# A two-block denoiser layer on one core: S5 kernel matrices turned where they are read, table copies moved to ScalarE, the last states copied by VectorE alone

## The chip, the core and the metric

The kernel runs on one core of a Trainium2 chip: TensorE (PE, matrix products), VectorE (DVE), ScalarE (ACT), GpSimd (POOL) and SyncE (SP), each with an instruction queue of its own that is worked off in order. SP does no arithmetic and only issues DMA transfers; ACT and POOL issue some too, and such an issue stands in their queue like any other instruction. The metric is the time of one execution on the device in microseconds (us).

## The reference, cut to what matters

Two blocks on 256 tokens of width 1024, float32 throughout. The first has two layers, latent attention (MLA) and an S5 state-space layer on 256 context and 256 latent tokens; the second block (attention and a gated convolution) follows and is left out here, since the change does not touch it.

```python
def _mla_mixer(h_lat, h_ctx, ...):          # layer 0: h = x * (1 + sc) + sh, then h @ w_in
    q_dn, kv_dn, k_rope, gate = split(h @ w_in)
    ...

def _s5_direction(u_ctx, u_lat, lam, dt, bmat, cmat):
    lam_bar = jnp.exp(lam * dt[:, None])
    b_bar = ((lam_bar - 1.0) / lam)[..., None] * bmat
    powers = jnp.exp(lam_dt[None] * jnp.arange(1, S5_CHUNK + 1))
    def step(h, u_chunk):
        bu = jnp.einsum('btgs,gps->btgp', u_chunk, b_bar)
        _, xs = lax.associative_scan(_ssm_combine, (a, bu), axis=1)   # x_t = lam_bar x_{t-1} + bu_t
        xs = xs + powers[None] * h[:, None]
        y = jnp.einsum('btgp,gsp->btgs', xs, cmat).real
        return xs[:, -1], y
    ...                                     # context first, its last state starts the latent tokens

def _s5_mixer(...):                         # layer 1, u, g = split(h @ w_in); 128 groups of 16 channels
    y = d_skip * u + forward direction + backward direction
    y = jax.nn.gelu(y)
    ya, yb = split(y @ w_glu + b_glu)
    return ((ya * sigmoid(yb)) * silu(g)) @ w_out
```

## The kernel before, in words

Large products are made either plainly in float32 (PE reads `raw`, the loaded weight) or as three products of split operands: ACT casts the weight to `whi` (L240), DVE subtracts to get `wlo` (L284), and PE takes hi*hi, hi*lo and lo*hi. Weights come from HBM in pieces of 512 KB into three rotating buffers each (`raw`, `whi`, `wlo`).

**Start (0 to 60 us).** The modulation vectors come from `in_wmod` (PE rows `b<-s,x`); DVE scales the tokens with them (`ready`, L483, eight instructions per half of the width); PE then makes the first columns of `h @ w_in` (`half`, rows `a<-s,raw` for the plain one and `a<-s,whi`, `a<-s,wlo` for the split ones). Beside that the tables of S5 are made: `tables()` reorders powers of `lam_bar` into `Em` (L988/L989, four copies on ACT) and `Fm` (L991/L992, four copies of 64x512 on POOL), and L993 copies `L4`. The list `HALVES` is the hand-written order of PE, SP and ACT in this stretch: "T0" calls `tables()` and then `ready(0)`, a number is a quarter of the products, "B" a part of the second half's modulation, "X" loads the second half of the tokens and "T1" makes it ready.

**S5 (about 530 to 789 us).** Time is cut into blocks of 4 tokens, so that the scan has 64 steps; within and between blocks the work is made of matrix products. Per m (0 to 15, eight groups each):

- *sums*: `inputs` makes u (PE `a<-s,raw`), ACT copies it to `Ub` (L1173) and writes it to HBM (`ud`), POOL reads it back as `U`; PE multiplies it with `BT` (`a<-U,whi`) and ACT copies the result to `Sc` (L1209, context) and to the `s` tiles (L1213, latent). DVE runs a tree over `Sc` (rows `sc<-LA,Sc` and `Sc<-Sc,sc`).
- *scan*: for each of four units, 63 steps on DVE (`ss<-x,s`, then twice `s<-s,ss`).
- *direct*: the part of y within a block. `s5_toeplitz` writes eight pieces of kernel matrices to HBM (`Td<-Kd`, issued by POOL). `kernel(m)` then loads 128x256 of it (`Ul<-Td`, POOL), ACT turns its two inner axes (`Ysb<-Ul`, L1339) and writes it back (`To<-Ysb`, issued by ACT). `direct(m)` loads u (`Ul<-ud`, SP) and two 64x4x64 blocks of `To` (SP) into one of two block-diagonal tiles `Tz` (named `x` in the profile) and PE multiplies (`c<-Ul,x`).
- *outputs*: two edge columns (L1256/L1257) and two copies of 64x16x63 states (L1262 forward, L1263 backward) into `H`, which is a `whi` buffer, three in all; PE multiplies with `CC` (`c<-whi,wlo`); for each pair of m ACT copies `Yb` (L1273) and writes it to HBM. `S5_DVE` says for which m the L1263 copy is made by DVE.
- *gates*: PE `b<-s,raw`, ACT `sg` (SiLU), written to HBM. *y(b)*: POOL loads `hl<-yd` once four m are done, ACT applies GELU and casts (`s<-hl`), DVE subtracts. *glu*: PE `a<-hl,raw` for the first three plainly, then split products (`a<-s,whi`), which fill the time from 789 us on.

`S5_PLAN` is the order in which these are written down; in S5 a scheduler at build time places each instruction in its engine's queue from that, by what is free when, so a change in one place moves others.

Of the kernel before, what the change touches and what calls it, by code (L numbers as in the profile page):

```python
# [19 lines left out]
P = 128  # L20
D = 1024
# [44 lines left out]
ORD = ("p", "d", "s")  # L66
KS = (0, 0)
KVP = True
HALVES = ("T0", "K4", 0, "B", 1, "B", 2, "B", 3, "X", "B", "T1")
S5_LATE = 16  # L70
LATE_AT = ()
SL1 = 1
# [10 lines left out]
S5_SPLIT = range(2, 8)  # L83
GLU_PLAIN = 3
GLU_EARLY = 6
S5_DVE = range(14, 16)
S5_UNITS = ((0,), (1,), (2,), (3,))

S5_PLAN = [("sums",0),("sums",1,(0,38)),("sums",2,(0,25),(1,25)),("sums",3,(1,25),(2,25)),("direct",0,4),("gates",0,5),("outputs",0,4),("scan",(1,13),(3,13)),("direct",4,8),("gates",5,13),("outputs",4,8),("direct",8,12),("scan",(2,38),(3,38)),("y",0,2),("gates",13,16),("outputs",8,12),("direct",12,16),("scan",(3,12)),("y",2,3),("glu",0,2),("outputs",12,16),("y",3,4),("glu",2,6)]
# [118 lines left out]
class Builder:  # L208
# [147 lines left out]
    def scratch(self):  # L356
        d = lambda shape, n: self.t(self.dp, shape, F32, n)
        self.BTd = d([16, P, 1024], "BTd")
        self.CCd = d([16, P, 1024], "CCd")
        self.Kd = d([P, 16, 112], "Kd")  # L360
        self.Td = d([P, 64, 64], "Td")
        self.To = d([P, 64, 64], "To")
        self.FEd = d([P, 2304], "FEd")
        self.LAd = d([P, 24, P], "LAd")
        self.sgd = d([16, P, NL], "sgd")
        self.ud = d([P, 16, 4, P], "ud")
        self.yd = d([P, 16, 4, 64], "yd")
# [101 lines left out]
    def mla_in(self):  # L469
# [7 lines left out]
        def ready(hf):  # L477

            kts = range(4 * hf, 4 * hf + 4)
            for kt in kts:  # L480
                for r in range(2):
                    sl = slice(r * NL, (r + 1) * NL)
                    nc.vector.tensor_scalar(xT[:, kt, sl], xT[:, kt, sl], self.sc(self.mod0, kt, r), self.sh(self.mod0, kt, r),  # L483
                                            op0=ALU.mult, op1=ALU.add)
            for kt in kts:
                self.h_last = self.split(hh[:, kt], hl[:, kt], xT[:, kt])
# [22 lines left out]
        with self.in_order(*ORD):  # L509
            fm = [self.mod_first(hf) for hf in range(2)]  # L510
            self.keep_busy(self.ones[256], KS[0])
            for _ in range(4):
                next(fm[0])
                self.keep_busy(self.ones[256], KS[1])
            load(0)
            for op in HALVES:
                if op == "T0":
                    next(fm[0])
                    self.tables()
                    ready(0)  # L520
                elif op == "B":
                    next(fm[1])
                elif op[:1] == "K" if isinstance(op, str) else False:
                    self.keep_busy(self.ones[256], int(op[1:]))
                elif op == "X":
                    load(1)
                elif op == "T1":
                    next(fm[1])
                    ready(1)
                else:  # L530
                    half(first[op], op, 0, KVP and op == 0)
# [386 lines left out]
    def s5_factors(self, keep, pre):  # L918
# [64 lines left out]

        f, b = slice(0, 64), slice(64, 128)
        gs = lambda x: x.rearrange("p s g -> p g s")
        def tables():
            for ri in range(2):
                nc.scalar.copy(Em[f, ri], gs(Lp[f, ri]))  # L988
                nc.scalar.copy(Em[b, ri], gs(Lp[b, ri, ::-1]))  # L989
            for ri in range(2):  # L990
                nc.gpsimd.tensor_copy(Fm[f, ri], gs(Q[f, ri, ::-1]))  # L991
                nc.gpsimd.tensor_copy(Fm[b, ri], gs(Q[b, ri]))  # L992
            nc.scalar.copy(L4, Lp[:, :, 3])  # L993
        L4 = self.t(keep, [P, 2, P])
        self.tables = tables
        return FE, L4
# [137 lines left out]
    def s5(self):  # L1134
# [98 lines left out]
        def direct(m):  # L1233

            if m % 2 == 0:
                pys["x"] = self.ps("c", (P, 2, 4, 64))
            py = pys["x"][:, m % 2]
            Ul = self.t(l1, [P, 4, 64], F32, "Ul", 3)
            nc.sync.dma_start(out=Ul, in_=udr[:, 4 * m:4 * m + 4, 0:64])
            T = Tz[m % TZ]  # L1240
            for j in range(2):
                rw = slice(64 * j, 64 * j + 64)
                nc.sync.dma_start(out=T[rw, :, rw], in_=self.To[rw, 4 * m:4 * m + 4])
            for q in range(4):
                self.mm(py[:, q], T[:, q], Ul[:, q], m % 2 == 0 and q == 0, False)
            pys[m] = pys["x"]

        def outputs(m):
# [10 lines left out]
            for x, D in enumerate(S):  # L1259
                n = D.shape[1]  # L1260
                k = min(n, 63 - n * x)
                nc.scalar.copy(H[f, :, :, 1 + n * x:1 + n * x + k], hv(D[f, :k, :, g]))  # L1262
                copy(H[b, :, :, 63 - n * x - k:63 - n * x], hv(D[b, k - 1::-1, :, g]))  # L1263
            py = pys.pop(m)
            for q in range(4):
# [46 lines left out]
        def sums(m0, m1):  # L1312
            for m in range(m0, m1):
# [11 lines left out]
                        n = 8 // len(TPM)  # L1325
                        self.s5_toeplitz(0, 16, range(n * i, n * i + n))
                yield from chunk_sums(m)
                for k in range(2 * m - 8, 2 * m - 6):
                    if 0 <= k < 16:
                        kernel(k)  # L1330

        def kernel(m):

            q = slice(4 * m, 4 * m + 4)
            a = self.t(l1, [P, 4, 64], F32, "Ul", 3)
            o = self.t(l1, [P, 4, 64], F32, "Ysb", 2)
            with self.tc.issue_after(self.u_read):
                nc.gpsimd.dma_start(out=a, in_=self.Td[:, q])
            nc.scalar.copy(o.rearrange("p q (o t) -> p q t o", t=4), a.rearrange("p q (t o) -> p q t o", t=4))  # L1339
            nc.scalar.dma_start(out=self.To[:, q], in_=o)  # L1340

        def take(it, n=1):
            for _ in range(n):
# [519 lines left out]
```

## Time and profile before

| | |
|---|---|
| time, median of 3 (lowest to highest) | 1420.02 us (1419.73 to 1423.65) |
| profiled execution: time, span in the trace | 1422.31 us, 1420.5 us |
| mean granted TensorE clock | 0.978 of 2.4 GHz |
| busy: PE, PEld | 1352.2 us (95%), 1151.5 us (81%) |
| busy: DVE, ACT, POOL | 1055.3 us (74%), 825.5 us (58%), 104.2 us (7%) |
| chain that ended last | PE 75%, ACT 8%, DMA 7%, DVE 6% |
| ... of it by line | DMA Ul<-Td 1%, ACT whi L1262 1%, ACT whi L1263 1% |

The span is the time from the first to the last recorded instruction; 1.8 us of the profiled execution lie outside it. PEld is TensorE's loading of weights, which overlaps its products. The chain is the work that ended last, followed back from the end: shares say on what the time hung, not how busy an engine was.

### The profile page before, as it was taken

The numbers are of one execution on the slowest core, as the hardware profiler recorded it, in microseconds if no ns is written. First come the engines' busy times: TensorE is split into PE (matmuls) and PEld (weight loads), VectorE is DVE, ScalarE is ACT, GpSimd is POOL, SyncE is SP. The second block draws the span as 40 slices with busy tenths as digits, with TensorE's granted clock in tenths as the row PEclk, the third lists the DMA queues.
The fourth block names the chain that finished last, engine by engine and source line by source line (L and its number), as shares of the span: only waits on it lengthen the run. The fifth ranks groups of instructions, "written<-read, shape, count | busy, mean of one in ns | idle before, by whom it ended". The sixth has DMA issues, their size and how long they took to land.

```text
span 1420.5 us, 26374 instructions
## 1 busy us (share of the span) xinstructions
PE 1352.2 (95%) x10042; PEld 1151.5 (81%) x10042; DVE 1055.3 (74%) x2546; ACT 825.5 (58%) x1429; POOL 104.2 (7%) x154
## 2 busy tenths in 40 slices
PE   5899999999999999888988999999999999999999
PEld 1577777877787666446877899999879999899999
DVE  7879768988689949899993465556667777688853
ACT  4598756665556943436368644445568664566642
POOL 3012100000011223210000000000100000000000
PEclk9999999999999989998999999999999999999999
DMA  8646533144275459764866766665433435565564
GB/s 310 223 164 223 186 126 117 56 130 145 82 263 184 151 159 313 212 190 139 245 207 203 251 206 191 198 187 180 158 116 122 146 126 163 171 185 180 184 186 135
DMA packets 105487, 252.60 MB, mean 178 GB/s; under 512 B 37168, under 2 KB 45744, under 8 KB 104976
## 3 DMA queue, kind: packets, MB, share of 16 engines
q1 hardware_dynamic: 77056, 204.50, 45.0%
q0 software_dynamic: 7344, 25.04, 5.7%
q10 hardware_dynamic: 20960, 21.37, 4.6%
q8 instruction: 79, 1.29, 0.4%
q14 instruction: 48, 0.39, 0.1%
HBM read 218.88 MB, written 34.08 MB: 178 GB/s over the span
## 4 chain that ended last, share of the span: by engine, by line
PE 75%; ACT 8%; DMA 7%; DVE 6%; issue 2%; ACTq 0%; SPq 0%; POOL 0%; POOLq 0%; DVEq 0%
PE a L228 59%; PE b L228 11%; PE c L228 2%; DMA ud<-Ub 1%; DMA s<-in_wmod 1%; ACT whi L240 1%; DMA Ul<-Td 1%; DVE wlo L284 1%; ACT whi L1262 1%; DVE bt L284 1%; PE c L669 1%; DMA raw<-in_w_glu 1%; ACT whi L1263 1%; ACT zc L1097 1%; DMA U<-ud 1%
## 5 line engine op out<-in xcount | busy, mean ns | idle before, releaser
L228 PE MATMUL a<-s,whi 128*128 128x256 f32 (+2 forms) x3024 | 645.1, 310 | 2.7 <-ACT whi L240 2.7
L228 PEld LDWEIGHTS a<-s,whi 128*128 128x128 f32 x3024 | 493.8, 191 | 34.3 <-issue 4.3
L228 PE MATMUL a<-s,wlo 128*128 128x256 f32 (+1 forms) x1512 | 464.1, 309 | 0.1
L284 DVE TENSOR_TENSOR wlo<-raw,whi 128x1024 fp32r<-128x1024 f32 (+2 forms) x234 | 280.8, 1201 | 195.3 <-ACT whi L240 192.7
L240 ACT CAST whi<-raw 128x1024 fp32r<-128x1024 f32 (+2 forms) x234 | 240.8, 1031 | 249.3 <-PE a L228 178.4
L228 PEld LDWEIGHTS a<-s,wlo 128*128 128x128 f32 x1512 | 289.0, 191 | 14.7 <-issue 0.9
L228 PE MATMUL a<-s,raw 128*128 128x512 f32 (+2 forms) x272 | 110.9, 559 | 17.6 <-ACT s L1213 6.5
L228 PEld LDWEIGHTS a<-s,raw 128*128 128x128 f32 x272 | 53.7, 203 | 64.3 <-issue 37.7
L284 DVE TENSOR_TENSOR s<-s,ss 128x64 f32<-128x64 f32 x504 | 88.8, 225 | 2.8 <-DVE s L284 0.2
L284 DVE TENSOR_TENSOR bt<-x,bc 128x512 f32<-128x512 f32 x128 | 83.5, 692 | 1.2
L228 PE MATMUL a<-x,whi 128*128 128x256 f32 (+1 forms) x384 | 74.2, 294 | 0.0
L284 DVE TENSOR_TENSOR ss<-x,s 128x128 f32<-128x128 f32 x248 | 63.1, 288 | 1.2
L228 PE MATMUL b<-s,raw 128*128 128x256 f32 x256 | 62.4, 404 | 1.3 <-ACT sg L1280 1.3
L228 PEld LDWEIGHTS a<-x,whi 128*128 128x128 f32 x384 | 60.4, 192 | 0.6
L228 PEld LDWEIGHTS b<-s,raw 128*128 128x128 f32 x256 | 51.0, 203 | 9.4 <-ACT sg L1280 1.7
L228 PE MATMUL a<-x,wlo 128*128 128x256 f32 (+1 forms) x192 | 56.1, 292 | 0.0
L284 DVE TENSOR_TENSOR sc<-LA,Sc 128x1024 f32<-128x1024 f32 (+5 forms) x96 | 44.3, 503 | 12.0 <-ACT Sc L1209 11.6
L284 DVE TENSOR_TENSOR Sc<-Sc,sc 128x1024 f32<-128x1024 f32 (+5 forms) x96 | 48.3, 503 | 0.4
L228 PEld LDWEIGHTS a<-U,whi 64*64 64x64 f32 x1024 | 32.3, 140 | 19.2 <-ACT Ub L1173 8.5
L731 DVE TENSOR_REDUCE st<-b 128x1 f32<-128x512 f32 (+1 forms) x64 | 34.8, 550 | 16.8 <-PE b L228 16.5
L228 PE MATMUL a<-U,whi 64*64 64x128 f32 x1024 | 37.5, 287 | 9.6 <-ACT Ub L1173 6.2
L240 ACT CAST s<-s 128x512 fp32r<-128x512 f32 (+1 forms) x48 | 25.9, 546 | 21.5 <-DVE s L284 15.0
(384 smaller groups left out, 2265.7 us busy)
## 6 DMA issues: line engine op xcount, KB each, us to landing
raw<-in_w_glu SPq DMA_DIRECT2D x64, 512.0 KB, 3.5
raw<-in_w_up SPq DMA_DIRECT2D x42, 512.0 KB, 3.5
raw<-in_w_out SPq DMA_DIRECT2D x40, 512.0 KB, 3.6
raw<-in_wmod SPq DMA_DIRECT2D x32, 512.0 KB, 3.6
raw<-in_w_u SPq DMA_DIRECT2D x32, 512.0 KB, 4.0
s<-in_wmod SPq DMA_DIRECT2D x16, 512.0 KB, 7.7
raw<-in_w_in SPq DMA_DIRECT2D x16, 512.0 KB, 4.2
BTd<-BT ACTq DMA_DIRECT2D x16, 512.0 KB, 3.4
```

Source lines behind the costliest of these rows:

```text
L228: self.last = self.ins(self.nc.tensor.matmul(out, l, r, start=start, stop=stop))
L240: self.nc.scalar.copy(hi, src)
L284: return self.ins(self.nc.vector.tensor_tensor(out, a, b, op=op))
L669: nc.tensor.transpose(pt[:, k, tt], pl[tt][:, (2 * b + k) * P:(2 * b + k + 1) * P], self.ident)
L731: nc.vector.tensor_reduce(st[:, 0:1], ps, axis=AX.X, op=ALU.max)
L1097: nc.scalar.copy(zt[f, :, 4:7], ct[f, :, 0:3])
L1262: nc.scalar.copy(H[f, :, :, 1 + n * x:1 + n * x + k], hv(D[f, :k, :, g]))
L1263: copy(H[b, :, :, 63 - n * x - k:63 - n * x], hv(D[b, k - 1::-1, :, g]))
```

## The change

Three edits. (1) `tables` takes a half: the `Em` copies stay at "T0"; the four `Fm` copies go from POOL to ACT and, with `L4`, to a new entry "F" of `HALVES` after the second quarter. (2) `kernel(m)` and the HBM tensor `To` go; `direct(m)` loads 128x256 of `Td` into `Ysb` (SP, two buffers), and two ACT copies of 64x4x4x16 turn it straight into the two diagonal blocks of `Tz`. (3) `S5_DVE` grows from m = 14, 15 to 12 to 15, and the forward copy obeys it as well, so all eight state copies of the last unit are on DVE.

```diff
-HALVES = ("T0", "K4", 0, "B", 1, "B", 2, "B", 3, "X", "B", "T1")
+HALVES = ("T0", "K4", 0, "B", 1, "F", "B", 2, "B", 3, "X", "B", "T1")
-S5_DVE = range(14, 16)
+S5_DVE = range(12, 16)
-        self.To = d([P, 64, 64], "To")
@@ mla_in
-                    self.tables()
+                    self.tables(0)
                     ready(0)
+                elif op == "F":
+                    self.tables(1)
@@ s5_factors
-        def tables():
+        def tables(hf):
             for ri in range(2):
-                nc.scalar.copy(Em[f, ri], gs(Lp[f, ri]))
-                nc.scalar.copy(Em[b, ri], gs(Lp[b, ri, ::-1]))
-            for ri in range(2):
-                nc.gpsimd.tensor_copy(Fm[f, ri], gs(Q[f, ri, ::-1]))
-                nc.gpsimd.tensor_copy(Fm[b, ri], gs(Q[b, ri]))
-            nc.scalar.copy(L4, Lp[:, :, 3])
+                if hf:
+                    nc.scalar.copy(Fm[f, ri], gs(Q[f, ri, ::-1]))
+                    nc.scalar.copy(Fm[b, ri], gs(Q[b, ri]))
+                else:
+                    nc.scalar.copy(Em[f, ri], gs(Lp[f, ri]))
+                    nc.scalar.copy(Em[b, ri], gs(Lp[b, ri, ::-1]))
+            if hf:
+                nc.scalar.copy(L4, Lp[:, :, 3])
@@ direct(m)
             T = Tz[m % TZ]
+            k = self.t(l1, [P, 4, 64], F32, "Ysb", 2)
+            nc.sync.dma_start(out=k, in_=self.Td[:, 4 * m:4 * m + 4])
             for j in range(2):
                 rw = slice(64 * j, 64 * j + 64)
-                nc.sync.dma_start(out=T[rw, :, rw], in_=self.To[rw, 4 * m:4 * m + 4])
+                nc.scalar.copy(T[rw, :, rw].rearrange("p q (o t) -> p q t o", t=4), k[rw].rearrange("p q (t o) -> p q t o", t=4))
@@ outputs(m)
-                nc.scalar.copy(H[f, :, :, 1 + n * x:1 + n * x + k], hv(D[f, :k, :, g]))
+                copy(H[f, :, :, 1 + n * x:1 + n * x + k], hv(D[f, :k, :, g]))
                 copy(H[b, :, :, 63 - n * x - k:63 - n * x], hv(D[b, k - 1::-1, :, g]))
@@ sums
-                for k in range(2 * m - 8, 2 * m - 6):
-                    if 0 <= k < 16:
-                        kernel(k)
-        def kernel(m):
-            q = slice(4 * m, 4 * m + 4)
-            a = self.t(l1, [P, 4, 64], F32, "Ul", 3)
-            o = self.t(l1, [P, 4, 64], F32, "Ysb", 2)
-            with self.tc.issue_after(self.u_read):
-                nc.gpsimd.dma_start(out=a, in_=self.Td[:, q])
-            nc.scalar.copy(o.rearrange("p q (o t) -> p q t o", t=4), a.rearrange("p q (t o) -> p q t o", t=4))
-            nc.scalar.dma_start(out=self.To[:, q], in_=o)
```

How the queues change at three places, word for word (line, operation, output<-input with buffer numbers, shape, count).

**Start, ACT.** Before, from the last `Em` copy to the second weight cast (`s_48` are the scaled tokens, `whi` the first quarters' weights):

```order
L989 COPY x_110<-x_148 64x512
L993 COPY x_188<-x_148 128x256
L240 CAST s_49_190<-s_48_189 128x512 x4
L240 CAST whi_284<-raw_282 128x512
L240 CAST whi_308<-raw_306 128x512
```

In the changed kernel, the same stretch:

```order
L995 COPY x_109<-x_147 64x512
L240 CAST s_48_189<-s_47_188 128x512 x4
L240 CAST whi_278<-raw_276 128x512
L991 COPY x_109<-x_168 64x512
L992 COPY x_109<-x_168 64x512
L991 COPY x_109<-x_168 64x512
L992 COPY x_109<-x_168 64x512
L997 COPY x_187<-x_147 128x256
L240 CAST whi_307<-raw_305 128x512
```

The four `Fm` copies now stand on ACT between the first and the second weight cast, behind the casts of the tokens; on POOL nothing stands in their place, and the two memsets `zb`, `zc` follow the first constants at once.

**Sums, ACT.** Before, where u of m = 8 is copied out (`Ub`), ahead of the sums of m = 6:

```order
L1173 COPY Ub_6066<-a_6055 128x512
L1339 COPY Ysb_5845<-Ul_5844 128x4x4x16
L1339 COPY Ysb_5850<-Ul_5849 128x4x4x16
L1174 DMA ud_93<-Ub_6066 128x512
L1340 DMA To_89<-Ysb_5845 128x256
L1340 DMA To_89<-Ysb_5850 128x256
L1209 COPY Sc_6071<-a_6074 128x128x2
```

After:

```order
L1177 COPY Ub_6045<-a_6034 128x512
L1250 COPY x_5325<-Ysb_7274 64x4x4x16 x2
L1250 COPY x_5326<-Ysb_7284 64x4x4x16 x2
L1178 DMA ud_92<-Ub_6045 128x512
L1213 COPY Sc_6050<-a_6053 128x128x2
```

and the loads that these copies wait for, on SP:

```order
L1246 DMA Ysb_7274<-Td_88 128x256
L1246 DMA Ysb_7284<-Td_88 128x256
L277 DMA raw_6333<-in_w_u 128x1024
L1246 DMA Ysb_7295<-Td_88 128x256
L1246 DMA Ysb_7305<-Td_88 128x256
L1200 DMA whi_6348<-BTd_85 128x1024
```

At the same place four turning copies stand where two copies and two writes stood. Of the other fourteen pieces that the sums turned and wrote back, four stay in the sums (one each ahead of the `Ub` copies of m = 10, 12 and 14, and one ahead of the last sums); ten move behind them, between gates and outputs. Weight loads of u (`raw<-in_w_u`) and of `BT` now queue behind `Ysb` loads on SP.

**Tail, ACT and DVE.** Before, on ACT, from the last unit's first state copy on:

```order
L1262 COPY whi_8539<-s_1401_6882 64x16x63
L1263 COPY whi_8539<-s_1401_6882 64x16x63
L1262 COPY whi_8562<-s_1401_6882 64x16x63
L1263 COPY whi_8562<-s_1401_6882 64x16x63
L1273 COPY Yb_8400<-c_7919 128x512
...
L1262 COPY whi_8588<-s_1401_6882 64x16x63
...
L1262 COPY whi_8611<-s_1401_6882 64x16x63
L1273 COPY Yb_8583<-c_8403 128x512
L240 CAST whi_8669<-raw_8667 128x1024
```

After, on ACT:

```order
L1280 COPY Yb_8343<-c_7858 128x512
L1263 COPY whi_8539<-x_6802 64x16
L1264 COPY whi_8539<-x_6802 64x16
L1281 DMA yd_93<-Yb_8343 128x8x64
L1250 COPY x_5325<-Ysb_8370 64x4x4x16 x2
L1250 COPY x_5326<-Ysb_8380 64x4x4x16 x2
L1263 COPY whi_8562<-x_6802 64x16
L1264 COPY whi_8562<-x_6802 64x16
L1280 COPY Yb_8534<-c_8346 128x512
L240 CAST whi_8620<-raw_8618 128x1024
```

and on DVE, right behind the last scan step:

```order
L284 TENSOR_TENSOR s_1368_6801<-s_1368_6801,ss_1694_8432 128x64 x2
L1269 COPY whi_8490<-s_1368_6801 64x16x63
L1270 COPY whi_8490<-s_1368_6801 64x16x63
L1269 COPY whi_8513<-s_1368_6801 64x16x63
L1270 COPY whi_8513<-s_1368_6801 64x16x63
L1269 COPY whi_8539<-s_1368_6801 64x16x63
```

Six state copies leave ACT's queue between the scan's end and the cast of the first split weight (`whi_8669`, now `whi_8620`); four turning copies (m = 14, 15) come in.

## Rows read from the trace of the kernel before

**Rows 1.** Busy time by stretch of the span: start and end in us, length, then for each engine its busy time and instruction count, the granted TensorE clock (1.00 is 2.4 GHz, 0.50 is 1.2 GHz), the share of the DMA engines' time, GB/s.

```profile
0.00:60.00 60.00, 39.95 (x148) 17.58 (x149) 43.96 (x99) 24.85 (x38) 13.85 (x22) 0.91 0.79 288
...
560.00:600.00 40.00, 32.35 (x248) 16.23 (x247) 34.40 (x120) 13.52 (x35) 10.27 (x16) 0.91 0.75 239
600.00:660.00 60.00, 50.90 (x509) 29.71 (x510) 58.28 (x242) 26.82 (x68) 10.93 (x14) 0.91 0.63 183
...
748.00:789.00 41.00, 34.07 (x356) 29.46 (x355) 12.48 (x43) 36.15 (x36) 0.41 (x1) 1.00 0.65 203
789.00:1420.00 631.00, 625.13 (x4868) 605.83 (x4868) 413.76 (x691) 344.30 (x570) 5.43 (x14) 0.99 0.55 171
```

**Rows 2.** TensorE's waits over the whole span: who waited, for what, us in total, times, the longest.

```profile
PE a L228 <- ACT s L1213: 8.5, 2, 6.5
PE a L228 <- ACT Ub L1173: 6.2, 3, 3.4
PE a L228 <- DVE s L483: 4.9, 1, 4.9
PE c L228 <- ACT whi L1263: 4.8, 3, 2.7
```

**Rows 3.** Time line of GpSimd and VectorE in the first 60 us: start, busy time of the row, engine, line, operation, tiles, count, and in brackets the idle time ahead of the row and what ended it.

```profile
20.99 1.31 POOL L991 COPY x<-x 64x512 f32<-64x512 f32 x1 [19.40 <-DVE x L284]
...
26.20 1.74 POOL L1052 MEMSET zc<- 128x1792 f32 x1
21.51 0.83 DVE L419 TENSOR_SCALAR x<-x 128x8 f32<-128x8 f32 x1
22.38 6.67 DVE L483 TENSOR_SCALAR s<-s,x 128x256 f32<-128x256 f32 x8
...
47.59 0.17 DVE L419 TENSOR_SCALAR x<-x 128x8 f32<-128x8 f32 x1
...
49.77 2.67 DVE L483 TENSOR_SCALAR s<-s,x 128x256 f32<-128x256 f32 x8
```

**Rows 4.** Time line of TensorE in the first 60 us, and one row of SyncE's DMA queue.

```profile
24.73 5.70 PE L228 MATMUL a<-s,raw 128*128 128x512 f32 x8 [4.94 <-DVE s L483]
...
42.56 1.64 PE L228 MATMUL b<-s,x 128*32 128x512 f32 x8
32.08 0.33 SPq L246 DMA_DIRECT2D raw<-in_w_in  x1
```

**Rows 5.** Time line of the S5 sums around 572 us: a row of GpSimd's DMA issues, ScalarE's copies and the DMAs that it issues (ACTq), TensorE, VectorE.

```profile
565.99 1.62 POOL L1338 DMA_DIRECT2D Ul<-Td  x3
570.95 0.65 ACT L1339 COPY Ysb<-Ul 128x256 f32<-128x256 f32 x1 [5.21 <-DMA Ul<-Td]
571.70 1.07 ACTq L1340 DMA_DIRECT2D To<-Ysb  x2
572.87 0.38 ACT L1209 COPY Sc<-a 128x256 f32<-128x256 f32 x1 [0.81 <-DVE Sc L284]
573.58 9.16 PE L228 MATMUL a<-s,raw 128*128 128x512 f32 x16 [6.54 <-ACT s L1213]
...
584.59 7.13 PE L228 MATMUL a<-s,raw 128*128 128x512 f32 x16
...
585.90 1.23 DVE L284 TENSOR_TENSOR sc<-LA,Sc 128x1024 f32<-128x1024 f32 x1 [4.52 <-ACT Sc L1209]
```

**Rows 6.** Groups of the stretch 556 to 790 us: line, engine, operation, tiles, count | busy time in us, mean ns of one | idle time ahead of them and what ended it. Below them, DMA issues of two stretches (545 to 600 and 600 to 665 us): count, KB each, median us from issue to landing.

```profile
L1262 ACT COPY whi<-s 64x1008 f32<-64x1008 f32 x16 | 31.4, 1960 | 2.7 <-DVE s L284 2.5
L1339 ACT COPY Ysb<-Ul 128x256 f32<-128x256 f32 x16 | 10.0, 660 | 37.1 <-DMA Ul<-Td 35.8 <-DMA To<-Ysb 1.2
L1263 DVE COPY whi<-s 64x1008 f32<-64x1008 f32 x2 | 2.0, 1024 | 17.4 <-PE c L228 17.4
Ul<-Td POOLq DMA_DIRECT2D x10, 128.0 KB, 3.7
Td<-Kd POOLq DMA_DIRECT2D x4, 256.0 KB, 8.0
Ul<-ud SPq DMA_DIRECT2D x6, 128.0 KB, 3.4
```

**Rows 7.** Time line at the second activation, 700 to 756 us: TensorE, ScalarE, VectorE.

```profile
725.82 1.33 PE L228 MATMUL c<-whi,wlo 128*64 128x64 f32 x18 [2.75 <-ACT whi L1263]
749.63 1.06 ACT L1289 ACTIVATE hl<-hl 128x1024 f32<-128x1024 f32 x1 [4.23 <-DMA hl<-yd]
751.15 1.43 DVE L284 TENSOR_TENSOR s<-hl,s 128x256 fp32r<-128x256 f32 x4 [3.95 <-ACT s L240]
```

**Rows 8.** Time line of the S5 tail, 748 to 789 us: TensorE, ScalarE, VectorE.

```profile
766.99 3.07 PE L228 MATMUL c<-whi,wlo 128*64 128x64 f32 x96
...
782.07 0.45 PE L228 MATMUL c<-whi,wlo 128*64 128x64 f32 x4 [1.16 <-ACT whi L1263]
...
788.85 0.51 PE L228 MATMUL a<-s,whi 128*128 128x256 f32 x2 [1.87 <-ACT whi L240]
774.21 1.96 ACT L1262 COPY whi<-s 64x1008 f32<-64x1008 f32 x1
...
787.76 1.04 ACT L240 CAST whi<-raw 128x1024 fp32r<-128x1024 f32 x1
775.96 1.03 DVE L1263 COPY whi<-s 64x1008 f32<-64x1008 f32 x1 [13.34 <-PE c L228]
```

## The prediction

> **What bounds the kernel now.** I read the stretches first [rows 1], then TensorE's waits [rows 2], then the time lines at the places of the three edits. From 789 us on TensorE is busy for 625.13 of 631 us: the end is bound by its work, and whatever it gains before 789 us should reach the end one for one. It loses time in two places: the first 60 us (39.95 busy) and the S5 layer (32.35 of 40, 50.90 of 60, and 34.07 of 41 in the tail). The three edits lie in these two places, but a removed wait counts only where its engine decides, so each needs its own stretch.
>
> **The start.** POOL copies the four `Fm` tables from 20.99 us on, then clears `zb` and `zc` until 27.94 [rows 3]. In just that time DVE slows down: the small L419 takes 0.83 us where the same instruction later takes 0.17, and the eight scalings L483 take 6.67 us where the same eight take 2.67 at 49.77. The product `a<-s,raw` waits for the second of them (4.94 us of idle TensorE), starts at 24.73 and takes 5.70 us [rows 4]. Afterwards TensorE runs without a gap worth naming to 42.56.
>
> **The sums.** `Ul<-Td`, `Ysb` and `To` form a trip through memory that ACT waits for: 35.8 us in all ahead of 16 `Ysb` copies [rows 6]. The first decides: its load is issued at 565.99, `Ysb` is copied at 570.95 after 5.21 us of waiting, ACT issues two writes until 572.77, and only then comes `Sc` at 572.87 [rows 5]. The profile puts that last wait of 0.81 us down to DVE, but the issue row ends exactly there. TensorE resumes at 573.58 after 6.54 us, and DVE runs dry later for 4.52 us. The later waits of this trip look costly (6.2 us of TensorE on `Ub` [rows 2]), yet between 600 and 660 us DVE is busy for 58.28 of 60 [rows 1]: its scan decides when the outputs may start, and TensorE would only wait for something else.
>
> **The tail.** From 774.21 us ACT copies states one after the other at about 1.95 us, until the first weight of the split products can be cast at 787.76 [rows 8]; it is busy for 36.15 of 41 us, DVE for 12.48 [rows 1]. DVE does the same copy in 1.02 us where ACT takes 1.96 [rows 6].
>
> **Cost of edit 1 (tables).** L419 gives back 0.83 - 0.17 = 0.66 and L483 6.67 - 2.67 = 4.00, so the scaled tokens are complete up to 4.7 us earlier. The first product needs two L483: 22.38 - 0.66 + 2 x 0.33 = 22.4, against 24.73, so TensorE starts some 2.3 us earlier, and that is what its unbroken run carries on. If the 5.70 us shrink as well (no stretch shows these eight products at the full clock without a wait), more comes; the load of 32.08, which waits for DVE's first `wlo`, moves along by four. ACT gets four copies of about 1.1 us, behind the casts of the tokens; the second weight cast is needed one quarter of products later, some 4 us, which covers them. Without that cover it would cost 4.4. Bounds 0 (the loads behind it decide, DMA share 0.79) and 4.7. I take 2.5.
>
> **Cost of edit 2 (turning).** The last `Td` pieces land 8.0 us after their issue [rows 6], about 565.5, where the trip of before starts too (565.99). Now SP loads 128 KB, which takes 3.4 us (`Ul<-ud`, SP) to 4.6 or more (`Ul<-Td`, 565.99 to 570.95; its median is 3.7): landed 568.9 to 570.1. Then four turning copies. A copy's length goes by what stands in one partition, 256 elements in both forms, so I take `Ysb`'s 0.66 each, 2.6 us for four, but the first two start when the first load lands, so 2.4 behind it; with one DMA issue of 0.5 (1.07 for two), `Sc` starts at 571.8 to 573.0, against 572.87. I take 0.5 earlier. In all, ACT loses 16 x 0.66 of `Ysb` and 16 issues of up to 0.5 (18.6 us) and gains 32 x 0.66 = 21.1; in the sums, where it is busy for 13.52 of 40 and 26.82 of 60 us, that is covered. What is left for the scan is the 60 - 58.28 = 1.7 us that DVE idles behind `Sc`; I take 0.7 of it.
>
> The Trainium skill ("DMA: Bandwidth & Descriptors", section "Anatomy of one DMA") puts a transfer at about 2.0 us plus its bytes at 436 GB/s, for 128 KB an estimate of 2.3 us. The trace disagrees by its medians of 3.4 to 3.7 for that size. By the page `Sc` would start at 565.5 + 2.3 + 2.4 + 0.5 = 570.7, 1.7 us earlier than I take.
>
> **Between scan and tail.** The second activation waits for its chain (outputs, `Yb`, `hl<-yd`): ACT 4.23 us ahead of `hl`, DVE 3.95 ahead of its cast, and the last steps of the scan stand behind that on DVE [rows 7]. TensorE's wait of 2.75 us at 725.82 for ACT's state copies belongs to the same chain. Ten turning pairs now stand on ACT here (10 x 1.3 = 13 us); they are covered where ACT waits for its inputs, and no writes to `To` are queued any more. Bounds 0 and 3.95; nearer the low end, as `hl<-yd` stays as it is: 0.4. So the last scan step comes 0.5 + 0.7 + 0.4 = 1.6 us earlier.
>
> **Cost of edit 3 (last states).** ACT loses six copies of 1.95 (11.7 us) and gets four turning copies (2.6). DVE gets six of 1.02 (6.1 us), in a stretch where it idles 28.5. A `whi` buffer comes free when its products are done (766.99 on), so the copies of m = 14, 15 still follow TensorE, now at about 2.1 us a pair instead of 3.9. Between 766.99 and 788.85 TensorE waited 1.16 and 1.87 us for ACT [rows 8], together 3.0. I take 2.3, since m = 15 must wait for a buffer of m = 12 and then for DVE's pair. Bounds 0 and 6.9, all that TensorE idles in the tail. If DVE's cover were gone, its six copies would cost 6.1.
>
> **Sum.** 2.5 + 1.6 + 2.3 = 6.4 us. Against the profiled execution: 1422.31 - 6.4 = 1415.9. That execution lies 2.3 us above the median of 1420.02, so the median becomes 1413.6.
>
> **Rival A, more passes through.** The 4.52 us of DVE behind `Sc` contain a product of 9.16 us that begins after 6.54 us of idle; the next sixteen of the same products took 7.13 [rows 5], so 2.0 us more come if TensorE isn't idle so long ahead of it. The tail gives all 6.9 instead of 2.3 (+4.6). The `Ysb` loads all land at the short end, 3.4 us instead of the middle of 4.0: 0.6. All three: 1413.6 - 7.2 = 1406.4; typical 1408.5. For it: `Ul<-Td` has 1% of the chain that ended last. Against: DVE's scan is full, and it takes what isn't tied to it. By the Trainium skill's fixed cost cited above (an estimate) the loads would be shorter still and this rival 1.1 us lower.
>
> **Rival B, little passes.** what slows DVE at the start need not be the copies: the eight L483 run on beside the memset `zc` at 26.20, and the memsets stay on POOL, if earlier; or the loads decide: edit 1 gives 0. And edit 2 only exchanges one wait for another. Left are 2.3 us: 1417.7, no measurable change (0.3%, 4.3 us, is about what this measurement can tell).
>
> **Rival C, slower.** The turning copies stand in ACT's queue directly ahead of `Ub` and `Sc`, at four further places of the sums. Each waits for a load on SP, which itself waits for the ACT copy that frees one of two `Ysb` buffers, and for TensorE to have read `Tz`. If one such round isn't early, it holds `Sc` for a load and a pair, 4.6 + 1.3 = 5.9 us, and a full DVE cannot make it up. One costs nearly the whole gain; more than 6.4 us of hold makes the kernel slower, three make 17.7 - 6.4 = 11.3: 1431. Against it: each load stands several sums ahead of its copies, and 35.8 us of the same waits in the old trip cost DVE only a few.
>
> **How the numbers follow.** Forecast 0.45 (1410.5 to 1416.7), A 0.20, B 0.21, C 0.14. Faster than 1415.8: most of the forecast (0.40), A, and a few of B, 0.66; same: 0.05 of the forecast and most of B, 0.21; slower: nearly all of C, 0.13. The range leaves out about one in ten on each side: the far end of A and edit 1 at its bound of 4.7 below (1406.4 - 2.2 = 1404, taken as 1403), and the larger part of C above (1422).
>
> **What would show it.** In the changed profile: L483 x8 at about 2.7 us and `a<-s,raw` starting near 22.5; no `Ysb` wait on ACT near 571, `Sc` near 571 to 572 after the start's shift; DVE's last scan step about 4 us earlier, start included; no state copies on ACT behind the last scan; the first `a<-s,whi` of `glu` near 782.4 (788.85 - 6.4). I am wrong if DVE's gaps in the sums grow, if L483 stays slow, or if ACT waits for `Ysb` ahead of `Ub`.

## The result and the profile after

The changed kernel takes 1409.26 us (median of 6; 1407.19 to 1414.61), the kernel before 1421.37 us (6 runs beside it): ratio 0.9916, 95% interval 0.9893 to 0.9939, that is 12.1 us or 0.8% faster. The prediction was 1413.6 us, range 1403 to 1422. Direction and range hold; the gain is nearly twice the 6.4 us of the sum. The profiled execution took 1408.22 us (span 1406.4), the one of before 1422.31 us.

Busy time by stretch, columns as in [rows 1]. The tail, 748 to 789 us before, now lies at 736 to 774 us.

```profile
0.00:60.00 60.00, 42.61 (x164) 20.56 (x165) 42.48 (x104) 32.00 (x45) 5.40 (x18) 0.91 0.79 293
560.00:600.00 40.00, 35.33 (x325) 19.56 (x324) 35.83 (x135) 15.65 (x43) 5.86 (x6) 0.91 0.63 175
600.00:660.00 60.00, 49.41 (x489) 31.18 (x488) 59.55 (x251) 27.50 (x59) 6.61 (x7) 0.91 0.51 144
736.00:774.00 38.00, 34.51 (x364) 30.08 (x362) 23.74 (x77) 29.05 (x37) 0.84 (x2) 1.00 0.69 225
774.00:1406.00 632.00, 624.94 (x4868) 606.09 (x4868) 414.06 (x691) 343.87 (x570) 4.74 (x13) 0.99 0.55 170
```

The last stretch is as long and as full as before (624.94 of 632, before 625.13 of 631): the whole gain arises ahead of it and reaches the end nearly one for one (the first split product comes 14.45 us earlier, the end of the span 14.1). In the tail ACT is no longer full (29.05 of 38, before 36.15 of 41).

The start (against [rows 3, 4]), VectorE and TensorE:

```profile
21.55 0.17 DVE L418 TENSOR_SCALAR x<-x 128x8 f32<-128x8 f32 x1
21.76 2.68 DVE L482 TENSOR_SCALAR s<-s,x 128x256 f32<-128x256 f32 x8
22.55 5.40 PE L228 MATMUL a<-s,raw 128*128 128x512 f32 x8 [3.32 <-DVE s L482]
```

The two DVE rows have the lengths that they have elsewhere beside an idle POOL, and TensorE starts 2.2 us earlier. The two memsets of GpSimd went out of the way as well: `zb` now stands ahead of this place and `zc`, which waits for the copy of `L4` (L997), behind it.

```profile
18.09 0.52 POOL L1056 MEMSET zb<- 128x512 f32 x1 [16.51 <-DVE sp L284]
30.50 1.60 POOL L1056 MEMSET zc<- 128x1792 f32 x1 [11.88 <-ACT x L997]
```

The sums (against [rows 5]): SP's loads, ScalarE, TensorE.

```profile
562.83 1.32 SPq L1246 DMA_DIRECT2D Ysb<-Td  x2
564.24 0.38 SPq L277 DMA_DIRECT2D raw<-in_w_u  x1
...
565.05 1.32 ACT L1250 COPY x<-Ysb 64x256 f32<-64x256 f32 x2 [3.67 <-DMA Ysb<-Td]
...
567.72 0.38 ACT L1213 COPY Sc<-a 128x256 f32<-128x256 f32 x1
...
566.51 1.08 PE L228 MATMUL c<-Ul,x 128*128 128x64 f32 x4 [3.83 <-ACT x L1250]
568.43 9.23 PE L228 MATMUL a<-s,raw 128*128 128x512 f32 x16 [0.84 <-ACT s L1217]
```

The wait has not gone: ACT waits 3.67 us for the load in place of 5.21, and TensorE 3.83 and 0.84 in place of 6.54. The sixteen products behind it take 9.23 us, no less than the 9.16 of before; the granted clock is at 0.50 for their first part:

```profile
568.00:572.00 4.00, 3.57 (x4) 1.51 (x5) 3.76 (x23) 2.03 (x8) 2.17 (x2) 0.50 0.80 255
```

Second activation and tail (against [rows 7, 8]): ScalarE, VectorE, TensorE.

```profile
740.19 1.06 ACT L1296 ACTIVATE hl<-hl 128x1024 f32<-128x1024 f32 x1
741.72 1.43 DVE L284 TENSOR_TENSOR s<-hl,s 128x256 fp32r<-128x256 f32 x4 [0.57 <-ACT s L240]
757.59 1.05 DVE L1269 COPY whi<-s 64x1008 f32<-64x1008 f32 x1 [4.41 <-PE c L228]
...
773.30 1.04 ACT L240 CAST whi<-raw 128x1024 fp32r<-128x1024 f32 x1
...
748.26 7.17 PE L228 MATMUL a<-hl,raw 128*128 128x256 f32 x32 [2.81 <-DMA raw<-in_w_glu]
755.37 3.07 PE L228 MATMUL c<-whi,wlo 128*64 128x64 f32 x96
774.40 0.50 PE L228 MATMUL a<-s,whi 128*128 128x256 f32 x2 [0.81 <-ACT whi L240]
```

The second cast (741.72) comes 9.4 us earlier than before, `c<-whi` x96 11.6, the first split product 14.45. A single execution scatters by some 3 us, so 14.45 is not to be read as the gain; the medians give 12.1. (The profiled execution of before lies 0.9 us above its median, that of the changed kernel 1.0 below.)

### The profile page after: what moved, and what is told of

Read it like the earlier page. It is cut to its first block, busy times and chain, and to the rows that moved or that the text cites. A ratio compares the mean times of both kernels' runs of the same rounds, so it can differ in the third digit from the quotient of the medians.

```text
span 1406.4 us, 26313 instructions
## 1 busy us (share of the span) xinstructions
PE 1341.9 (95%) x10042; PEld 1145.8 (81%) x10042; DVE 1056.9 (75%) x2552; ACT 826.9 (59%) x1441; POOL 87.3 (6%) x134
## 4 chain that ended last, share of the span: by engine, by line
PE 69%; DVE 11%; ACT 10%; DMA 6%; issue 3%; ACTq 0%; SPq 0%; POOL 0%; DVEq 0%; POOLq 0%
PE a L228 56%; PE b L228 9%; DVE bt L284 2%; PE c L228 2%; DVE s L284 2%; ACT whi L240 1%; DVE wlo L284 1%; DMA s<-in_wmod 1%; DVE sc L284 1%; DVE Sc L284 1%; ACT zc L1101 1%; DVE ss L284 1%; PE c L670 1%; ACT zc L1098 1%; ACT whi L1270 1%
## 5 line engine op out<-in xcount | busy, mean ns | idle before, releaser
L228 PE MATMUL a<-s,raw 128*128 128x512 f32 (+2 forms) x272 | 108.0, 548 | 9.4 <-DMA FEd<-x 5.2
L228 PEld LDWEIGHTS b<-s,raw 128*128 128x128 f32 x256 | 49.7, 199 | 11.6 <-ACT sg L1287 4.2
L284 DVE TENSOR_TENSOR sc<-LA,Sc 128x1024 f32<-128x1024 f32 (+5 forms) x96 | 44.2, 499 | 10.8 <-ACT Sc L1213 10.5
L1177 ACT COPY Ub<-a 128x512 f32<-128x512 f32 x14 | 8.2, 586 | 70.0 <-PE a L228 70.0
```

Source lines behind the costliest of these rows:

```text
L228: self.last = self.ins(self.nc.tensor.matmul(out, l, r, start=start, stop=stop))
L284: return self.ins(self.nc.vector.tensor_tensor(out, a, b, op=op))
L1177: nc.scalar.copy(u, ps.rearrange("p (r s c) -> p s r c", r=2, s=4))
```

## The experiments

All were timed in five rounds beside the kernel before. The first three each make one edit alone.

**Edit 1 alone (tables).** The diff is its hunk of `HALVES`, `tables` and `s5_factors` above.

> Edit 1 alone (table copies to ScalarE) on the kernel before; the queues of TensorE, VectorE and SyncE keep their order. Theory: the start's gain is passed on one for one, so the last product ahead of the first gap (c<-x,raw, 44.88 us before) comes at about 41.5 and the end 2.5 to 3.4 us earlier, about 1418.4 us. Rival: something between 60 and 789 us gives it back and the end does not move (1421.4).

1419.23 us, ratio 0.9986 (0.9969 to 1.0003). **Edit 2 alone (turning)**, the hunks of `To`, `direct` and `kernel`:

> Edit 2 alone (kernel matrices turned where they are read, no To) on the kernel before. Theory: it earns most of the rest by itself: Sc about 1.9 us earlier, the scan's first end 2.8 earlier, the second activation 6 earlier, end near 1421.4 - 6 = 1415.4 us. Rival: the scan and the activation gained in the changed kernel only because the start came earlier and met other transfers; alone it gives the 1.6 us of the prediction, 1419.8 us.

1417.71 us, ratio 0.9975 (0.9960 to 0.9991), between theory and rival. **Edit 3 alone (last states)**, `S5_DVE` and the forward copy:

> Edit 3 alone (the last unit's eight state copies on VectorE) on the kernel before. Theory: ScalarE's serial copies set the tail, so the first split product comes 2.3 to 2.9 us earlier, 1418.8 us. Rival: the tail hangs on the second activation and on the loads of w_glu, and ScalarE would only wait: no change, 1421.4 us.

1419.13 us, ratio 0.9988 (0.9971 to 1.0005). Alone, the three gain 2.3, 3.8 and 2.4 us, together 8.5; made together they gain 12.1. Of the three only edit 2's gain is clear of noise by these times. Hence the next run, edits 2 and 3 without edit 1 (before with those hunks only), and the changed kernel once more beside it:

> Edits 2 and 3 without edit 1 (the table copies back on POOL at the start). Theory (edits 2 and 3 depend on each other): edit 2 alone brought the last scan step about 7.4 us earlier than before (762.6 to 757.2), but from the last c<-whi product group to the first split product of glu it took 26.4 us instead of 21.9, because ACT now also had the last turning copies; edit 3 alone shortened that stretch to 18.6 us. Together the group should start near 759.3 and the split products some 19 us later, near 778.3 instead of 788.85: about 10 us faster than before, 1411 us. Rival (the edits add up): 1421.5 - 3.8 - 2.4 = 1415.3 us, with the first split product near 782.

> The changed kernel itself, once more beside the three variants of it that run with it, so that these are compared on one chip. Expected: 1407 to 1411 us (1409.26 was the median so far).

1411.13 us, ratio 0.9934 (0.9910 to 0.9958), 10.9 us faster than before; the group of 96 started at 759.12 and the first split product at 778.15, as the theory had it (759.3 and 778.3), not as the sum of the two (782). By the time alone the sum, 1415.3 us, is not excluded: the interval reaches 1416.0. (The expectation's 7.4 us for the last scan step is a slip: from 762.6 to 757.2 it is 5.4; the group of 96 came 7.7 us earlier.) The changed kernel again took 1410.25 us (0.9923, 0.9896 to 0.9949). The five traces and the two of the result, by stretch (worked out from the start times of the rows: the last `Ub` copy ahead of the first direct product, the `Sc` copy behind it, `hl<-hl` of the second activation, the group `c<-whi` x96, the first `a<-s,whi` of `glu`):

| us | start to `Ub` | `Ub` to `Sc` | `Sc` to `hl` | `hl` to `c<-whi` x96 | x96 to `a<-s,whi` |
|---|---|---|---|---|---|
| before | 565.15 | 7.7 | 176.8 | 17.4 | 21.9 |
| edit 1 | 563.04 | 7.5 | 175.2 | 20.0 | 22.6 |
| edit 3 | 566.34 | 7.1 | 178.2 | 18.6 | 18.6 |
| edit 2 | 565.09 | 5.3 | 173.8 | 15.1 | 26.5 |
| edits 2, 3 | 562.90 | 6.8 | 172.6 | 16.8 | 19.0 |
| all | 560.80 | 6.9 | 172.5 | 15.2 | 19.0 |
| all, again | 561.00 | 6.8 | 172.0 | 15.1 | 19.0 |

By the means of the rows with an edit and without it: edit 1 brings `Ub` 3.3 us earlier (564.9 to 561.6); edit 2 shortens the next two stretches by 0.9 (7.4 to 6.5) and 4.0 (176.7 to 172.7). It shortens the stretch behind `hl` too, by 2.0 us (17.1 to 15.1, without the clock losses told below). With the loads of `To` gone SP starts the first two weights of `glu` 9.5 and 3.0 us ahead of `hl<-yd` instead of beside it, and so sixteen plain products run ahead of the activation instead of two. SP and TensorE, before:

```profile
741.39 2.29 SPq L1303 DMA_DIRECT2D raw<-in_w_glu  x2
748.38 0.59 PE L228 MATMUL a<-hl,raw 128*128 128x256 f32 x2
749.95 7.17 PE L228 MATMUL a<-hl,raw 128*128 128x256 f32 x32 [0.97 <-DMA raw<-in_w_glu]
```

and after:

```profile
725.86 0.33 SPq L1310 DMA_DIRECT2D raw<-in_w_glu  x1
732.37 0.33 SPq L1310 DMA_DIRECT2D raw<-in_w_glu  x1
737.42 3.62 PE L228 MATMUL a<-hl,raw 128*128 128x256 f32 x16
741.30 4.15 PE L228 MATMUL a<-hl,raw 128*128 128x256 f32 x18 [0.27 <-ACT hl L1296]
```

In the last stretch the edits do not add up. Edit 3 alone shortens it by 3.3 us (21.9 to 18.6), edit 2 alone lengthens it by 4.6 (to 26.5), and with both it is 2.8 shorter (19.0). So edit 2 needs edit 3: without it ACT, which now also turns m = 14, 15 there, holds TensorE (2.67 us for a state copy at 777.08, 1.10 for a turning copy at 780.21).

With edit 1 alone it is the clock that takes the gain back, in the stretch behind `hl` (17.4 becomes 20.0). TensorE's row and the stretches around it (columns as in [rows 1]), edit 1 alone:

```profile
755.56 10.17 PE L228 MATMUL a<-hl,raw 128*128 128x256 f32 x32 [2.93 <-DMA raw<-in_w_glu]
```
```profile
752.60:755.50 2.90, 0.04 (x1) 0.00 (x0) 2.56 (x11) 2.88 (x2) 0.00 (x0) 0.89 0.84 278
755.50:758.00 2.50, 2.44 (x6) 1.99 (x7) 2.19 (x10) 2.47 (x2) 0.00 (x0) 0.50 0.26 103
```

and the kernel before, at the same wait:

```profile
757.00:759.80 2.80, 0.12 (x1) 0.00 (x0) 2.46 (x11) 2.78 (x2) 0.00 (x0) 1.00 0.89 260
759.80:762.00 2.20, 2.12 (x10) 1.88 (x11) 1.93 (x9) 2.16 (x3) 0.00 (x0) 1.00 0.39 153
```

Before, TensorE idles 2.76 us for a weight and the clock stays at 1.00; with edit 1 alone it idles 2.93 us at the same place, the clock falls to 0.50 (1.2 GHz), and the 32 products take 10.17 us instead of 7.17. These 3.0 us are nearly all that this trace loses behind `hl` (3.3). Edit 3 alone shows the same (8.86 us behind a wait of 2.82), and so do edits 2 and 3 together:

```profile
750.33 8.86 PE L228 MATMUL a<-hl,raw 128*128 128x256 f32 x32 [2.72 <-DMA raw<-in_w_glu]
```

**The load of `Ysb` issued by POOL (e4).**

```diff
-            nc.sync.dma_start(out=k, in_=self.Td[:, 4 * m:4 * m + 4])
+            nc.gpsimd.dma_start(out=k, in_=self.Td[:, 4 * m:4 * m + 4])
```

> The changed kernel with one difference: the sixteen Ysb<-Td loads are issued by GpSimd instead of SyncE; the order of TensorE, VectorE and ScalarE stays. Theory Q (the issuing queue makes the short load): they land about 4.7 us after issue as Ul<-Td did, Sc in the sums starts 2.4 us later than in the changed kernel and the end comes at about 1411.7 us. Theory T (lighter traffic makes it): they land in about 2.3 to 2.8 us from GpSimd too and the end stays at 1409.3 us within 0.7.

1413.93 us, ratio 0.9952 (0.9938 to 0.9967): 3.7 to 4.7 us of the gain gone, more than theory Q had it (1411.7). GpSimd's and SP's issues, ScalarE:

```profile
562.71 1.09 POOL L1246 DMA_DIRECT2D Ysb<-Td  x2
...
561.21 0.33 SPq L277 DMA_DIRECT2D raw<-in_w_u  x1
563.18 0.32 SPq L1200 DMA_DIRECT2D whi<-BTd  x1
...
568.79 1.30 ACT L1250 COPY x<-Ysb 64x256 f32<-64x256 f32 x2 [6.99 <-DMA Ysb<-Td]
```

The load is issued at the same time as in the changed kernel (562.83), but arrives 6.1 us later instead of 2.2: SP, which no longer holds it, has started two weight loads of 512 KB. Is it POOL or the weights? **The first two `Ysb` loads on SP, behind the weight load (e6)** (`wl` is the handle of `raw<-in_w_u`):

```diff
-            nc.sync.dma_start(out=k, in_=self.Td[:, 4 * m:4 * m + 4])
+            with self.tc.issue_after(self.wl["w_u", 11]) if m < 2 else ExitStack():
+                nc.sync.dma_start(out=k, in_=self.Td[:, 4 * m:4 * m + 4])
```

> The changed kernel with the first two Ysb loads still on SP, but behind the weight load raw<-in_w_u that followed them. Theory (a place ahead of the 512 KB weight loads is what makes the load short): the Ysb loads land 3.5 to 5 us after their issue instead of 2.2 to 2.4, the first turning copy and Sc come 1 to 2.5 us later (Sc near 569 to 570 instead of 567.72), and the end is 1411 to 1412. Rival (SP's queue alone makes it short, wherever the load stands in it): they land after 2.4 us again, and the end stays at 1409 to 1410.

1409.91 us, ratio 0.9917 (0.9893 to 0.9942): as the changed kernel. SP, ScalarE and TensorE, then a stretch with its granted clock:

```profile
561.07 0.33 SPq L279 DMA_DIRECT2D raw<-in_w_u  x1
562.21 6.98 SPq L1249 DMA_DIRECT2D Ysb<-Td  x3
562.13 0.38 ACT L1215 COPY Sc<-a 128x256 f32<-128x256 f32 x1 [0.46 <-PE a L228]
567.53 2.66 ACT L1253 COPY x<-Ysb 64x256 f32<-64x256 f32 x4 [4.17 <-DMA Ysb<-Td]
562.89 7.13 PE L228 MATMUL a<-s,raw 128*128 128x512 f32 x16
...
746.39 8.86 PE L228 MATMUL a<-hl,raw 128*128 128x256 f32 x32 [2.78 <-DMA raw<-in_w_glu]
```
```profile
748.00:750.00 2.00, 2.00 (x6) 1.61 (x5) 1.77 (x7) 1.98 (x2) 0.00 (x0) 0.50 0.00 0
```

The load takes 5.3 us on SP too, a little more than expected, so a place on SP does not make it short. That GpSimd's queue does not make it long shows in the kernel before, in the same 128 KB on that queue, `Ul<-Td` issued at 575 and at 589 us:

```profile
Ul<-Td POOLq DMA_DIRECT2D x2, 128.0 KB, 5.3
Ul<-Td POOLq DMA_DIRECT2D x2, 128.0 KB, 2.9
```

The first pair starts with a weight load of SP (575.21), the second 4.1 us behind the last one (584.74). So it is the weights started just ahead, not the queue's owner. It is no strict rule: a pair at 619.50, 1.2 us behind a weight load, took 3.3 to 3.4 us. The time does not do as expected, for a reason that I had not seen: the scheduler moved the turning copies behind the `Sc` copies, so `Sc` comes at 562.13, TensorE doesn't wait, and its sixteen products take 7.13 us in place of 9.23. The first state copy, behind the first unit's scan, comes 2.6 us earlier (644.41 against 647.03), and most of this is lost again at 746.39, where the clock fell as above (8.86 instead of 7.17).

**The `Td` pieces one place earlier (e9).**

```diff
-TPM = (1, 2, 3, 4)
+TPM = (0, 1, 2, 3)
```

> The changed kernel with the four pairs of Td<-Kd pieces written one place earlier in the sums (0 to 3 instead of 1 to 4); the scheduler then puts the first Ysb loads on SP ahead of two more loads of BT, and turning copies one place earlier on ACT. Theory (the last Td pair, issued at 552.99 and landed about 9 us later, is what holds the first Ysb loads until 562.83): the last pair is issued near 542.5, the first Ysb loads near 552 to 554, TensorE's wait of 3.83 us at 566.5 goes, and DVE's trees start up to 4 us earlier: 1405 to 1408 us. Rival (the sums are held by DVE and by the weight loads, and the load only moves): Sc starts within 1 us of 567.7 and the end stays at 1408.5 to 1410.5; if SP is held by the earlier Ysb loads ahead of BT, TensorE waits for whi instead and it is slower, up to 1413.

1415.97 us, ratio 0.9958 (0.9939 to 0.9977): 5.7 us slower than the changed kernel beside it. ScalarE, TensorE, VectorE:

```profile
558.36 2.61 ACT L1250 COPY x<-Ysb 64x256 f32<-64x256 f32 x4 [11.29 <-DMA Ysb<-Td]
561.63 1.97 PE L228 MATMUL a<-U,whi 64*64 64x128 f32 x28 [7.35 <-ACT Ub L1177]
564.60 2.36 DVE L284 TENSOR_TENSOR sc<-LA,Sc 128x1024 f32<-128x1024 f32 x2 [7.47 <-ACT Sc L1213]
```

Neither theory: the loads do start earlier (554.98), but the copies now stand ahead of a `Ub` copy, wait 11.29 us there, and hold `Ub`, TensorE and DVE. This is rival C's mechanism, and the total is near its price for one round (5.9 us), though TensorE and DVE each wait over 7 us here.

**Why is `hl<-yd` shorter?** DMA issues around the second activation: count, KB each, median us from issue to landing. The kernel before:

```profile
hl<-yd POOLq DMA_DIRECT2D x1, 512.0 KB, 6.7
```

and the changed one:

```profile
hl<-yd POOLq DMA_DIRECT2D x1, 512.0 KB, 4.2
```

It took 6.7, 6.4 and 7.1 us in the three kernels with `To` (before, edit 1, edit 3) and 4.1 to 4.9 in all eleven without, those that are told further down included. Two trials at the cause, **the `Ysb` loads in 256-byte pieces** (as `To` was read) and **the first `glu` weights issued late**:

```diff
-            k = self.t(l1, [P, 4, 64], F32, "Ysb", 2)
+            k = self.t(l1, [P, 4, 72], F32, "Ysb", 2)[:, :, :64]
```

> The changed kernel with a gap of 8 elements behind each 64 of an Ysb tile, so that its load falls into 4 pieces of 256 bytes a partition instead of one of 1 KB (8192 pieces in all instead of 2048); bytes, queues and the work of all engines stay. Theory (the small pieces of To, in and out, were what made loads long in the kernel before): the first Ysb loads land 4 to 5 us after their issue instead of 2.2 to 2.5, Sc comes 2 us later, the load hl<-yd takes 6.4 to 7 us as in the three kernels with To instead of 4.1 to 4.9, DVE waits 2 to 3.5 us at the second activation, and the end is 1412 to 1414 us. Rival (the size of the pieces doesn't matter here): 2.4 us and 4.1 to 4.9 us again, and the end stays at 1409 to 1410.5.

```diff
-                    for e in range(2):
+                    with self.tc.issue_after(self.ul[14]) if m == 0 else ExitStack():
+                      for e in range(2):
                         nc.sync.dma_start(out=self.raws[e]...
```

> The changed kernel with both weight loads raw<-in_w_glu of the first plain glu product issued behind the u load of m = 14, that is some 0.5 us behind hl<-yd, as in the kernel before, where both were issued within 1.5 us of it; in the changed kernel they are issued 9.5 and 3 us ahead of it. Theory (the weight loads that start with hl<-yd are what made it long): hl<-yd lands 6.4 to 7.1 us after its issue instead of 4.1 to 4.9, the second activation and its casts come 2 to 3 us later, and the end is 1411 to 1413 us. Rival (they have no part in it): it lands after 4.1 to 4.9 us; TensorE's first plain product then still starts later, and the end is 1409.5 to 1411.

Small pieces: 1412.66 us, ratio 0.9936 (0.9914 to 0.9959), `hl<-yd` 4.7 us, `Sc` at 567.77 as in the changed kernel. The `Ysb` load itself took 4.1 us, as the theory had it, but its neighbours with whole pieces took up to 4.0, so this one trace does not tell. Late weights: 1411.89 us (0.9931, 0.9913 to 0.9948), `hl<-yd` 4.1 us; the weights were issued at 737.74, 2.8 us behind it, not the 0.5 that I meant, so this does not test the theory. It does show what late weights cost TensorE: it waits 5.31 us for them at 742.99 and has made none of the plain products by then. Neither makes `hl<-yd` long, and neither median is separable from the changed kernel's. In the three kernels with `To` two weight loads are issued between 1.8 us ahead of `hl<-yd` and 0.8 us behind it; in ten of the others one, 1.7 to 3.4 us ahead, and the next 2.2 us behind it or later; with late weights none ahead. Two weight loads sharing the transfer are thus the likely cause, in line with e4 and e6, but that is argued, not shown; the loads of `To` that run beside it in the same three kernels are not ruled out.

**The plain products of `glu` with their inner loops exchanged**, on the kernel of e6 (e12) and on the changed one (e13):

```diff
-                    for k in range(k0, k1):
-                        for e in range(2):
+                    for e in range(2):
+                        for k in range(k0, k1):
```

> The kernel of e6 (first Ysb loads behind the weight load) with the two inner loops of the plain glu products exchanged, so that one weight buffer is free 8 products earlier and its next load starts some 2 us earlier. Theory (with the scan earlier, the wait for raw<-in_w_glu and the fall of the granted clock behind it take e6's gain away): TensorE's wait of 2.78 us at 746.39 falls below 1 us, the clock stays at 1.00, the c<-whi group of 96 starts near 753 instead of 755.2, and the end is 1407 to 1408.5 us. Rival (ACT's state copies, which end near 752.4, or something later decide): the group starts at 754 or later and the end stays at 1409 to 1410.

> The changed kernel with the same exchange of loops alone. Theory: its wait of 2.7 us for raw<-in_w_glu near 748 falls below 1 us, but the c<-whi group of 96 can start only when ACT's state copies end (near 753.8), so it gains at most 1 us: 1408.5 to 1409.5 us. Rival (the load doesn't start earlier, since TensorE has one weight to wait for in any order): no change, 1409 to 1410.

1407.15 us (ratio 0.9900, 0.9879 to 0.9921) and 1409.51 us (0.9913, 0.9891 to 0.9936). TensorE in the first:

```profile
740.82 16.67 PE L228 MATMUL a<-hl,raw 128*128 128x256 f32 x76 [2.00 <-ACT hl L1299]
757.42 3.07 PE L228 MATMUL c<-whi,wlo 128*64 128x64 f32 x96
```

The wait for the weight is gone and the clock stays at 1.00, but the group of 96 comes at 757.42, not near 753: the scheduler put 18 more plain products ahead of it (12 are left behind it, 30 in the changed kernel). It has the lowest median of all, 2 to 3 us under the changed kernel, but the intervals overlap, so it is not shown to be faster; its first split product, at 773.97, is only 0.4 us earlier. The exchange alone changes nothing that these times show.

## Why the prediction came out as it did

**Edit 1: 2.5 us taken, 3.3 measured** (the bound was 4.7). The step was right: with the copies on POOL the eight L483 take 6.65 to 6.67 us in four traces, without them 2.67 to 2.68 in three, and `a<-s,raw` starts at 22.55, near the 22.4 worked out. The 3.3 us are there at the end of that run of products: `c<-x,raw` starts at 44.2 to 44.9 us in the four traces and at 40.5 to 41.5 in the three. The times alone do not show edit 1: by itself its interval reaches 1.0003, and on top of edits 2 and 3 it gives 0.9 to 1.9 us. Not all of DVE's delay came from the copies, though; the first and the fifth of the eight L483 before, taken out by themselves:

```profile
22.38 1.19 DVE L483 TENSOR_SCALAR s<-s,x 128x256 f32<-128x256 f32 x1
26.33 1.76 DVE L483 TENSOR_SCALAR s<-s,x 128x256 f32<-128x256 f32 x1
```

Beside each of three `Fm` copies an L483 took 1.19 or 1.20 us, beside `zb` 0.69 and beside `zc` 1.76; after, all eight take 0.41. With L419 the copies thus held DVE for some 3.0 us and the memsets for some 1.6. What the first product needs hung on the copies alone; but half of rival B's doubt was just, and that the memsets left this place too was not foreseen. Behind the casts the `Fm` copies cost nothing that can be seen.

**Edit 2 at `Sc`: 0.5 taken, 0.9 measured.** The forecast that one wait is exchanged for another is what the rows show. The load took 2.2 to 4.1 us in the eight kernels where no weight load of 512 KB starts just ahead of it, median 3.5; I had 3.4 to 4.6. The estimate of 2.3 us from the Trainium skill ("DMA: Bandwidth & Descriptors", "Anatomy of one DMA"), which I set aside, was met in one trace, the profiled one of the result (2.2); it is the short end here. The Trainium skill gives that sum there for transfers that GpSimd issues, and `Ysb` is loaded by SP; GpSimd's loads of this size took 2.6 to 5.3 us in the kernel before (`Ul<-Td`, median 3.1). Behind weight loads it took 5.3 to 6.1 (three kernels).

**Edit 2 behind `Sc`: 0.7 + 0.4 = 1.1 taken, 4.0 + 2.0 = 6.0 measured.** This step failed. For the DVE stretch I took 0.7 of 1.7 us; with `Sc` at hand earlier DVE is busy for 59.55 of 60 us. From `Sc` to the first state copy behind the first unit's scan the three kernels with `To` took 80.3 to 82.2 us, the four without 78.8 to 80.2: 1.8 by the means. Another 2.2 us are the second activation. I kept to the low end of 0 to 3.95 there "as `hl<-yd` stays as it is"; it did not stay: 6.7 us became 4.2, and the wait of DVE fell from 3.95 to 0.57. The last 2.0, behind `hl`, I had put at nothing: with the weights of `glu` started earlier, more of the plain products lie ahead of the activation. Removing thirty-two loads of `To` from SP changed when SP starts the weights; that this is also what made `hl<-yd` short is likely, not shown.

**Edit 3: 2.3 taken, 2.8 measured** (the bound was 6.9). The term counted the four turning copies that edit 2 brings into the tail, so it is to be held against both edits: 21.9 to 19.0 us. Mechanism and size were right: ACT's serial copies set this stretch, and TensorE's two waits for them, 3.0 us, were its price. Edit 3 alone gives 3.3 there; the bound, all of TensorE's idle time in the tail, was far off. What I had not said is that edit 2 without edit 3 loses 4.6 us here.

**The sum.** By stretch 3.3 + 0.9 + 4.0 + 2.0 + 2.8 = 13.0 us, between the 12.1 of the medians and the 14.45 of the profiled pair. Of the 6.6 us by which the forecast's 6.4 falls short of this, 4.9 are edit 2 behind `Sc`.

**The signs.** L483 and `a<-s,raw` came as foretold, and none of the three signs of being wrong did. Of the last unit's state copies none is on ACT any more, but two of the unit before still follow the last scan step there (757.12 and 759.11). The wait for `Ysb` did not go (3.67 us). "`Sc` near 571 to 572" does not follow from the sum's own terms (572.87 - 2.5 - 0.5 = 569.9); it came at 567.72, the last scan step 9.4 us earlier instead of 4, the first split product at 774.40 instead of 782.4.

**The rivals.** A (1406.4 to 1408.5) is nearer to the result than the forecast, but by luck, since its terms are not what gave the gain: from the group of 96 on the tail gave 2.8 us, not 6.9, the loads took 3.4 us in the median as A had it but 2.0 to 5.3 each, and its 2.0 us for the product are not in this kernel (9.23 us). Its mechanism for that product is right: the clock is at 0.50 behind the idle TensorE, and in the kernel of e6, where TensorE does not wait, the product takes 7.13. B's total is out, though half of its doubt about the start was just. C's wait doesn't occur here but does, at about its price, when the `Td` pieces are moved.

## What to carry to other kernels

When several edits lie on one chain, price the stretch with the others in place: a tail that one engine fills takes back what is gained ahead of it, so an edit tried alone can look worth almost nothing. A short load can take longer when large ones were started just ahead of it, on its own queue or another (`Ysb`: 5.3 to 6.1 us against 2.2 to 4.1). Loads that are removed from a queue let the ones behind them start earlier, and that can be worth more than the removed waits: look at what is issued next. And a short wait of TensorE can cost twice, for itself and for the clock of the products behind it.

## What the hardware showed unexpectedly

Waits of the same length at the same place had different ends. Eleven of the kernels make the same 32 plain products behind a wait for `raw<-in_w_glu`. Behind 2.68, 2.69, 2.73, 2.76 and 2.81 us of idle TensorE (all again, e9, edit 2, before, all) the clock stayed at 1.00 and they took 7.17 us; behind 2.72, 2.78, 2.79, 2.82, 2.83 and 2.93 (edits 2 and 3, e6, small pieces, edit 3, e4, edit 1) they took 8.82 to 10.17 us, with the clock at 0.50 for part of them. The two sets overlap, so the length of the wait alone does not decide; what does stays open.
